# A decoder layer on one core: FFN tile 0 as plain products, partial sums of the other tiles in PSUM, and a final norm without GpSimd

## The chip, the core and the metric

The kernel runs on one core of a Trainium2 chip. The core's engines, as the profile names them, are TensorE (PE for matmuls and transposes, PEld for its weight loads), VectorE (DVE), ScalarE (ACT), GpSimd (POOL) and SyncE (SP, which here issues the DMAs). PE writes into PSUM banks; DVE and ACT read them. Each engine works through its own queue in order and waits on the others by semaphores. The metric is the device time of one execution, in microseconds (us).

## What is computed

One layer of a hybrid decoder on 512 tokens of width 1024, in float32. The part that the change touches is the last third:

```python
    x = x + jnp.concatenate([y_attn, y_ssd, y_pool], axis=-1) @ w_out
    h = rmsnorm(x, norm_ffn)
    gate, up = jnp.split(h @ w_gate_up, 2, axis=-1)
    return x + (jax.nn.silu(gate) * up) @ w_down
...
    return rmsnorm(x, norm_final)
```

`FFN_HIDDEN` is 2816, so the feed-forward part (FFN) has 22 tiles of 128 hidden units. What comes ahead (a norm, the input projection, block-sparse attention, a state-space scan and a pooling mixer) is the same in both kernels.

## The kernel before

**Precision.** Every float32 operand is split into a high part (a copy by ACT into the matmul type) and a low part (source minus high part, on DVE; `hi_lo`, lines 809 and 810). `mm3` issues three matmuls for one product of 128 rows: high x high (line 166), high x low (167) and low x high (168). So every product counts three times.

**The boundary.** The output projection writes `po0` and `po1` (512 columns each) for four token tiles t of 128 tokens. `add_x1` (766) adds them to x on DVE, `square` (774) gives the row sums on ACT, `row_rstd` (780 to 787) turns them into the norm's factor by a short chain of 128x1 instructions on DVE with a Sqrt on ACT in it. `h2_lane(t)` then makes `xh` (932, two halves on DVE), has PE transpose it into two banks `ps_h` (939, eight transposes), and splits the banks into `h2_hi` (950, ACT) and `h2_lo` (951, DVE). Token tiles 2 and 3 also make the sums `t1` to `t4` of four quadrants of the normalised rows (966 to 974, DVE), each split into a high and a low part (962, 963); three of them are the operands `T2`, `T3`, `T4`, the fourth goes in place of a quadrant of `h2_hi`.

**The tiles.** For each hidden tile, gate and up, for both halves of the tokens (256 each) and both halves of the inner dimension (512 each), are computed by a Strassen-Winograd scheme: seven products instead of eight, of four steps x three matmuls of 256 columns, so 12 matmuls each and 84 for a tile. They are numbered 1, 2, 6, 7, 5, 4, 3, in that order (`pair_order`). Their weights are a gate tile (products 1 and 2), a half of an up tile (4), and sums of those (`add_up`, 856 to 859, on DVE): `sa` for 5 and 6, `sb` for 7 and 3. `block` issues one product into its half of a bank (`psf1`, `psf2`, `psf7`, `psf5`, `psf4`; 2 and 6 share one, 4 and 3 another). `block_out` adds up: ACT copies product 1 out (1064), DVE does six adds in a buffer `E` (1059: one of 512 columns, five of 256), ACT does one Silu over 512 columns (1080), DVE the product (1081), and `hi_lo` makes `aTh` and `aTl`.

**Groups.** Tiles come in the groups of `GROUPS`: 0 to 3, 4 to 7, 8 to 11, 12 to 15, 16 and 17, 18 to 21. After each the down projection multiplies the group's tiles into `pd` (512 columns, four token tiles, two output halves h) and DVE adds that to x. In the first group, products 1 and 2 of tiles 0, 1 and 2 (`FIRST`, line 38) stand ahead of the rest, since they need only the first 256 tokens.

**The end.** The last half of the last group is `pdl`, token tile by token tile, the last one in two parts of 256 columns. Each is added to x on DVE (1169), squared on ACT (1172), multiplied by the final norm's weights `gf` on GpSimd (1151 for the left half, 1174 for the right), given its factor by `row_rstd`, scaled on ACT (left, 1180) and DVE (right, 1182), and written by two DMAs from SP (1181, 1183).

**What sets the order.** A scheduler places each instruction in its engine's queue by program order, with those under `high_priority` ahead. Weight loads (512 KB each, four raw buffers) and their splits are drawn from the list `plan` by `advance`, one or more after each product, when a slot is free and the load has landed by the planner's own clock. `issue_after` forces an instruction behind a given one. `H2_DELAY` (39) is how far each `h2_lane` waits on the planner's clock before its transposes.

## Time and profile before

| | |
|---|---|
| median of 3 runs (lowest to highest) | 577.88 us (576.05 to 577.88) |
| the profiled execution, device time | 577.72 us |
| its span in the profile | 576.0 us |
| PE busy | 557.9 us, 3492 matmuls and transposes |
| DVE busy | 463.0 us |
| ACT busy | 281.0 us |
| GpSimd busy | 60.1 us |
| data read from and written to memory | 58.93 MB, 2.11 MB |

The span is the time from the first to the last instruction that the profiler records. "Busy" counts the time in which an engine works, not the time in which it waits for a semaphore. Matmuls overlap in the pipeline: each shows its full duration (0.28 us for 256 columns), and the next one starts 0.12 us after it. So PE's pace is read from starts, not from durations.

### The profile page before, as it was taken

Reading aid. Unit: us, or ns where it says so; the run is one execution under the profiler, and the core shown is the slowest. Engines: PE = TensorE matmul, PEld = TensorE weight load, DVE = VectorE, ACT = ScalarE, POOL = GpSimd, SP = SyncE. Lnnn points to the kernel's source line nnn. Section 1 sums busy time; section 2 is a strip of 40 time slices with the busy share of each in tenths; the row PEclk is TensorE's granted clock in tenths of the full one; section 3 lists DMA queues with packets and bytes.
Section 4 is the critical chain, followed back from the end, with each engine's and each line's share of the span. In section 5 each row is a group of like instructions: output and inputs, shape, how many; then the busy total and the mean of one; then the engine's idle time right before and its main releaser. Section 6 shows DMA issues by size and latency. Waiting matters only on the chain.

```text
span 576.0 us, 9083 instructions
## 1 busy us (share of the span) xinstructions
PE 557.9 (97%) x3492; PEld 501.6 (87%) x3492; DVE 463.0 (80%) x838; ACT 281.0 (49%) x481; POOL 60.1 (10%) x75
## 2 busy tenths in 40 slices
PE   7999999999998997999999999999999999999994
PEld 4998998888776886998899989998899889899984
DVE  4387966899989768999899968897689877798445
ACT  5686554667646546464345522643155324325234
POOL 6011002006860000000000000000000000000033
PEclk8999999999999998999999999999999999999998
DMA  7862233422122701245324321443034233222003
GB/s 238 296 209 75 74 109 110 129 75 86 43 75 73 292 0 38 74 126 175 138 75 147 115 106 47 156 128 110 0 121 162 85 109 110 75 73 75 1 0 146
DMA packets 19519, 61.62 MB, mean 107 GB/s; under 512 B 2300, under 2 KB 3476, under 8 KB 19476
## 3 DMA queue, kind: packets, MB, share of 16 engines
q1 hardware_dynamic: 19476, 61.05, 31.6%
q8 instruction: 27, 0.44, 0.3%
q14 instruction: 16, 0.13, 0.1%
HBM read 58.93 MB, written 2.11 MB: 106 GB/s over the span
## 4 chain that ended last, share of the span: by engine, by line
PE 61%; DVE 7%; ACT 1%; issue 1%; DVEq 0%; ACTq 0%
PE psf L166 12%; PE psf L168 11%; PE psf L167 11%; PE pd L166 6%; PE pd L167 6%; PE pd L168 6%; PE po L166 2%; PE po L167 2%; PE po L168 2%; PE ps_h L939 1%; DVE sl L810 1%; DVE E L1059 1%; DVE x L1169 0%; DVE sz L528 0%; ACT sqf L1172 0%
## 5 line engine op out<-in xcount | busy, mean ns | idle before, releaser
L167 PE MATMUL pd<-dl,aTh 128*128 128x512 f32 x160 | 63.3, 395 | 0.0
L166 PE MATMUL pd<-dh,aTh 128*128 128x512 f32 x160 | 62.8, 396 | 0.0
L168 PE MATMUL pd<-dh,aTl 128*128 128x512 f32 x160 | 60.8, 395 | 0.0
L1059 DVE TENSOR_TENSOR E<-psf,E 128x256 f32<-128x256 f32 x110 | 42.4, 418 | 11.2 <-PE psf L168 10.3
L166 PE MATMUL psf<-h_hi,gh 128*128 128x256 f32 x176 | 49.9, 285 | 0.1
L167 PE MATMUL psf<-h_lo,sh 128*128 128x256 f32 x176 | 49.7, 282 | 0.0
L167 PE MATMUL psf<-h_lo,gh 128*128 128x256 f32 x176 | 49.7, 283 | 0.0
L168 PE MATMUL psf<-h_hi,gl 128*128 128x256 f32 x176 | 49.6, 282 | 0.0
L168 PE MATMUL psf<-h_hi,sl 128*128 128x256 f32 x176 | 49.5, 281 | 0.0
L166 PE MATMUL psf<-h_hi,sh 128*128 128x256 f32 x176 | 49.5, 281 | 0.0
L138 DVE TENSOR_TENSOR wlo<-raw,whi 128x1024 fp32r<-128x1024 f32 (+3 forms) x29 | 33.6, 1159 | 18.0 <-ACT whi L137 17.9
L1151 POOL TENSOR_TENSOR x<-x,gf 128x512 f32<-128x512 f32 x4 | 5.1, 1294 | 359.5 <-ACT sqf L774 359.5
L137 ACT ACTIVATE whi<-raw 128x1024 fp32r<-128x1024 f32 (+3 forms) x34 | 31.6, 931 | 22.0 <-PE pc L167 10.0
L166 PE MATMUL pc<-hT_hi,whi 128*128 128x512 f32 x104 | 41.3, 397 | 0.0
L809 ACT ACTIVATE sh<-sb 128x1024 fp32r<-128x1024 f32 x22 | 23.2, 1056 | 36.3 <-PE pd L167 29.8
L168 PE MATMUL pc<-hT_hi,wlo 128*128 128x512 f32 x104 | 40.9, 393 | 0.0
L167 PE MATMUL pc<-hT_lo,whi 128*128 128x512 f32 x104 | 40.8, 392 | 0.0
L766 DVE TENSOR_TENSOR x<-pd,x 128x512 f32<-128x512 f32 x44 | 28.4, 686 | 14.9 <-PE pd L168 14.8
L809 ACT ACTIVATE dh<-r_d 128x1024 fp32r<-128x1024 f32 x22 | 23.1, 1057 | 33.9 <-PE psf L167 22.6
L168 PEld LDWEIGHTS pd<-dh,aTl 128*128 128x128 f32 x160 | 30.1, 188 | 7.3
L166 PEld LDWEIGHTS pd<-dh,aTh 128*128 128x128 f32 x160 | 30.1, 188 | 7.0
L167 PEld LDWEIGHTS pd<-dl,aTh 128*128 128x128 f32 x160 | 30.1, 188 | 6.9
(291 smaller groups left out, 1714.3 us busy)
## 6 DMA issues: line engine op xcount, KB each, us to landing
r_g<-wgu SPq DMA_DIRECT2D x22, 512.0 KB, 3.7
r_u<-wgu SPq DMA_DIRECT2D x22, 512.0 KB, 3.9
r_d<-wd SPq DMA_DIRECT2D x22, 512.0 KB, 3.2
raw<-w SPq DMA_DIRECT2D x13, 512.0 KB, 3.5
raw<-wo SPq DMA_DIRECT2D x8, 512.0 KB, 3.2
rawx<-xT SPq DMA_DIRECT2D x8, 256.0 KB, 3.8
rawn<-xn SPq DMA_DIRECT2D x4, 512.0 KB, 5.1
x<-xn SPq DMA_DIRECT2D x4, 512.0 KB, 7.2
```

The source lines that it names most:

```text
L137: nc.scalar.activation(hi[:, sl], raw[:, sl], AF.Copy)
L138: eng.tensor_tensor(lo[:, sl], raw[:, sl], hi[:, sl].bitcast(F32), ALU.subtract)
L166: nc.tensor.matmul(ps, s_hi, m_hi, start=first, stop=False)
L167: nc.tensor.matmul(ps, s_hi, m_lo, start=False, stop=False)
L168: nc.tensor.matmul(ps, s_lo, m_hi, start=False, stop=last)
L766: nc.vector.tensor_tensor(x1[t][:, cs], ps, x1[t][:, cs], ALU.add)
L809: nc.scalar.activation(hi, src, AF.Copy)
L810: eng.tensor_tensor(lo, src, hi.bitcast(F32), ALU.subtract)
L939: nc.tensor.transpose(pst[:, j * P : (j + 1) * P], xh[:, kt * P : (kt + 1) * P], ident)
L1059: nc.vector.tensor_tensor(o_, a_, b_, ALU.add)
L1151: nc.gpsimd.tensor_tensor(x1[t][:, :512], x1[t][:, :512], gf[0][:, :512], ALU.mult)
```

## The change

**Tile 0 plain.** Tile 0 is computed as eight plain products: `g0`, `u0` (gate and up of the first 256 tokens) and `g1`, `u1` (the other half), each of 24 matmuls of 256 columns into banks `pspg` and `pspu`. The new order of the first group is g0, u0 of tile 0, then products 1 and 2 of tiles 1, 2 and 3, then g1, u1, then the rest. Their weights need only the split, no sums. The loads come in the same order.

**The boundary.** All four token tiles now split both halves into `h2_hi` and `h2_lo` and copy both out, `xh` has two buffers, the sums of quadrants are made in place and are no longer under `high_priority`, and the fourth sum has an operand `T1` of its own (product 5 reads it).

**Sums in PSUM.** In tiles 1 to 21 products 1, 6, 7 and 4 are accumulated in one bank `psB`, one after the other; products 5 and 3 likewise in `psC`; product 2 has `psA`. ACT copies the partial sum out of `psB` after product 1 (`u1`), 6 (`u2`) and 7 (`u3`); DVE adds each of them once to another bank. The Silu is done in two halves of 256 columns. `pair_order` puts products of the next tile between those of a tile, and products 4 and 3 of a group's last tile go into the down projection, ahead of its second tile.

**The end.** The products with `gf` move from GpSimd to DVE, on the right into the scaling itself. The factor's chain (`last_rstd`) lets the Sqrt read the sum of squares with scale and bias, so that one step ahead of it falls away. The Sqrt's table is loaded right behind the last Silu (`pre2`). The left half's DMA is issued from ACT's queue, the right half of the last token tile goes in two parts, and the last matmuls are held in program order.

The diff, cut to its core:

```diff
-FIRST = [(i, n) for i in range(3) for n in (1, 2)]
-H2_DELAY = (10.0, 5.0, 3.0, 3.0)
...
+PLAIN = (0,)
+EARLY = (1, 2, 3)
+FIRST = (
+    [(i, n) for i in PLAIN for n in ("g0", "u0")]
+    + [(i, n) for i in EARLY for n in (1, 2)]
+    + [(i, n) for i in PLAIN for n in ("g1", "u1")]
+)
+H2_DELAY = (7.0, 5.0, 5.0, 5.0)
...
+        def left_out(t, r):
+            nc.scalar.activation(x1[t][:, :512], x1[t][:, :512], AF.Copy, scale=r)
+            nc.scalar.dma_start(out[t * P : (t + 1) * P, :512], x1[t][:, :512])
+
+        def last_rstd(t):
+
+            y = tiny.tile([P, 1], F32, name=f"rsfy{t}", tag="rsy")
+            v = tiny.tile([P, 1], F32, name=f"rsfv{t}", tag="rsv")
+            a = tiny.tile([P, 1], F32, name=f"rsfa{t}", tag="rsa")
+            root[t] = nc.scalar.activation(y, ss[:, t, 1:2], AF.Sqrt, scale=1.0 / D, bias=ss[:, t, 0:1]).ins
+            nc.vector.scalar_tensor_tensor(v, ss[:, t, 1:2], -0.5 / D, sh[:, t : t + 1], ALU.mult, ALU.add)
+            nc.vector.reciprocal(y, y)
+            nc.vector.tensor_scalar(a, y, y, v, ALU.mult, ALU.mult)
+            nc.vector.tensor_scalar(y, a, 1.5, y, ALU.add, ALU.mult)
+            return y
...
-                if gi == 0 and i == 0:
-                    stages[3:3] = [("wx", 2, split_g, 1), ("wx", 2, split_g, 2)]
-                elif gi == 0 and i in (1, 2):
+                if i in PLAIN:
+                    stages = [("wx", 2, split_plain, i, "g"), ("wx", 2, split_plain, i, "u")]
+                    if i == PLAIN[-1]:
+                        stages += [("wx", 2, split_g, k) for k in EARLY]
+                elif i in EARLY:
                     stages = stages[1:]
...
+
+            f_ = {1: b11, 3: b12, 2: b22, 4: b21}
+
+            def out_(n):
+                d_hi, d_lo = T[n][0][:, :, cs], T[n][1][:, :, cs]
+                nc.scalar.activation(d_hi, f_[n], AF.Copy)
+                return nc.vector.tensor_tensor(d_lo, f_[n], d_hi.bitcast(F32), ALU.subtract)
+
+            nc.vector.tensor_tensor(b11, b11, b12, ALU.subtract)
+            nc.vector.tensor_tensor(b12, b22, b12, ALU.subtract)
+            nc.vector.scalar_tensor_tensor(b22, b11, -1.0, b22, ALU.mult, ALU.subtract)
+            out_(2)
+            nc.vector.scalar_tensor_tensor(b21, b22, -1.0, b21, ALU.mult, ALU.subtract)
+            out_(3)
+            last = out_(1)
+            out_(4)
             crit.append(last.ins)
...
-                        h2_split(t, 1, b22)
+                for b in range(2):
+                    p3 = h2_bank(t, b, xh)
+                    h2_split(t, b, p3)
+                    h2_copy(t, b, p3)
+            mark(f"h2_{t}", 0.5)
             if t >= 2:
                 yield when("T")
-                with tc.high_priority():
-                    if t == 2:
-                        h2_sums(t, h2f[2, 0], h2f[2, 1])
-                    else:
-                        h2_sums(t, b12, b22)
-                        h2_split(t, 1, b22)
-            mark(f"h2_{t}", 0.5)
+                h2_sums(t)
+                mark(f"T_{t}", 0.5)
...
-        def block_out(i, n, e, ps):
-            if n == 1:
-                e["p1"] = fw.tile([P, 256], F32, name=f"p1_{i}", tag="p1", bufs=3)
-                nc.scalar.copy(e["p1"], ps)
...
+            gl, gr, ur = slice(0, 256), slice(256, 512), slice(256, 512)
+            if n in (1, 6, 7):
+                u_ = e["u1" if n == 1 else "u2" if n == 6 else "u3"] = (fw if n == 1 else ap_).tile(
+                    [P, 256], F32, name=f"u{n}_{i}", tag=f"u{n}", bufs=len(EARLY) + 1 if n == 1 else 2
+                )
+                nc.scalar.copy(u_, e["B"])
+            elif n == 2:
+                e["g"] = fw.tile([P, S], F32, name=f"g{i}", tag="g", bufs=4)
+                add(e["g"][:, gl], e["A"], e["u1"])
+                nc.scalar.activation(e["g"][:, gl], e["g"][:, gl], AF.Silu)
+            elif n == 4:
+                e["a"] = e.get("a") or ap_.tile([P, S], F32, name=f"a{i}", tag="a")
+                nc.vector.scalar_tensor_tensor(e["a"][:, :256], e["B"], -1.0, e["g"][:, gl], ALU.mult, ALU.mult)
...
+                add(e["g"][:, gr], e["C"], e["u2"])
+                last = nc.scalar.activation(e["g"][:, gr], e["g"][:, gr], AF.Silu)
+                if i == FT - 1:
+
+                    with tc.issue_after(last.ins):
+                        nc.scalar.activation(tiny.tile([P, NT], F32, name="pre2", tag="pre"), rstd, AF.Sqrt)
+                nc.vector.scalar_tensor_tensor(e["a"][:, ur], e["ur"], -1.0, e["g"][:, gr], ALU.mult, ALU.mult)
+                out_aT(i, e["a"])
                 st.pop(i)
+            if n in (5, 7) and "u3" in e and "C" in e:
+                e["ur"] = ap_.tile([P, 256], F32, name=f"ur{i}", tag="ur")
+                add(e["ur"], e["C"], e["u3"])
...
+            which = {1: "B", 6: "B", 7: "B", 4: "B", 2: "A", 5: "C", 3: "C"}[n]
+            new = which not in e
+            if new:
+                e[which] = bank(f"ps{which}_{i}")[:, :256]
+            ps = e[which]
             for kt in range(4):
                 sl = slice(kt * P, (kt + 1) * P)
-                mm3(ps, w_hi[:, sl], w_lo[:, sl], *moving(n, kt), kt == 0, kt == 3)
+                mm3(ps, w_hi[:, sl], w_lo[:, sl], *moving(n, kt), new and kt == 0, kt == 3, chain=not new)
...
+        def block_plain(i, what):
+
+            which, half = what[0], int(what[1])
+            need((i, which))
+            w_hi, w_lo = ops[i, which]
+            if (i, which) not in plain:
+                plain[i, which] = bank(f"psp{which}_{i}")
+            ts_ = slice(half * 256, (half + 1) * 256)
+            for kt in range(KT):
+                sl = slice(kt * P, (kt + 1) * P)
+                mm3(plain[i, which][:, ts_], w_hi[:, sl], w_lo[:, sl], h2_hi[:, kt, ts_], h2_lo[:, kt, ts_], kt == 0, kt == KT - 1)
+            if half:
+                ops.pop((i, which))
+                done("wx", 2)
+
+        def plain_out(i):
+            g = fw.tile([P, S], F32, name=f"g{i}", tag="g", bufs=4)
+            a_ = ap_.tile([P, S], F32, name=f"a{i}", tag="a")
+            nc.scalar.activation(g, plain[i, "g"], AF.Silu)
+            nc.vector.tensor_tensor(a_, plain[i, "u"], g, ALU.mult)
+            out_aT(i, a_)
...
-            return [(i, n) for i in range(lo_, hi_) for n in (1, 2, 6, 7, 5, 4, 3)]
+
+            tiles = [i for i in range(lo_, hi_) if i not in PLAIN]
+            order = []
+            for i, nxt in zip(tiles, tiles[1:] + [None]):
+                if (i, 6) not in order:
+                    order += [(i, n) for n in (1, 2, 6, 5, 7) if (i, n) not in order and (i, n) not in FIRST]
+                if nxt is None:
+                    return order, [(i, 4), (i, 3)]
+                if nxt in EARLY:
+                    order += [(nxt, 6), (i, 4), (nxt, 5), (i, 3), (nxt, 7)]
+                else:
+                    order += [(nxt, 1), (i, 4), (nxt, 2), (i, 3)]
...
-                seq = FIRST + [q for q in seq if q not in FIRST]
+                seq = FIRST + seq
             for j, q in enumerate(seq):
-                if gi == 0 and j == 6:
+                if q == (PLAIN[0], "g1"):
                     ensure("h2_2", "h2_3")
+                if gi == 0 and j == len(FIRST):
+                    ensure("T_2", "T_3")
                     L.drain()
-                    tfctx.close()
                     bctx.close()
                     ap_ = fpool("aT", 2)
-                block(*q)
+                    for i in PLAIN:
+                        plain_out(i)
...
+                            if h == 0 and k == lo_ + 1:
+                                for q in tail:
+                                    block(*q)
...
-                            nc.gpsimd.tensor_tensor(x1[t][:, :512], x1[t][:, :512], gf[0][:, :512], ALU.mult)
+                            nc.vector.tensor_scalar_mul(sh[:, t : t + 1], ss[:, t, 0:1], -0.5)
+                            nc.vector.tensor_tensor(x1[t][:, :512], x1[t][:, :512], gf[0][:, :512], ALU.mult)
...
+                                with tc.issue_after(pd_end):
+                                    pd_end = mm3(ps[:, part], aT[k][0][:, ts_], aT[k][1][:, ts_], w_hi[:, js], w_lo[:, js], k == lo_, k == hi_ - 1)
...
-                            r = row_rstd(t, "rsf")
-                        nc.scalar.activation(x1[t][:, :512], x1[t][:, :512], AF.Copy, scale=r)
-                        nc.sync.dma_start(out[t * P : (t + 1) * P, :512], x1[t][:, :512])
-                        nc.vector.tensor_scalar_mul(x1[t][:, 512:], x1[t][:, 512:], r)
-                        nc.sync.dma_start(out[t * P : (t + 1) * P, 512:], x1[t][:, 512:])
+                            r = last_rstd(t)
+                            if t > 0:
+                                with tc.issue_after(root[t]):
+                                    left_out(t - 1, rs[t - 1])
+                            rs[t] = r
+                            for part in parts:
+                                os_ = slice(512 + part.start, 512 + part.stop)
+                                nc.vector.scalar_tensor_tensor(x1[t][:, os_], x1[t][:, os_], r, gf[0][:, os_], ALU.mult, ALU.mult)
+                                nc.sync.dma_start(out[t * P : (t + 1) * P, os_], x1[t][:, os_])
+                            if t == NT - 1:
+                                left_out(t, r)
```

Three places of the order of instructions, first the kernel before, then the changed one; in the names, the digits right behind the letters are the token tile or the hidden tile, and the last number is a buffer's.

DVE at the boundary, between the transposes of token tile 2 and the second half of `xh` of tile 3 (`tf`, `T2l` to `T4l` are the sums and their low parts of tile 2). Before:

```order
L963 TENSOR_TENSOR h2_lo_2096<-tf12_2377,h2_hi_2095 128x4x128
L963 TENSOR_TENSOR T3l_2367<-tf32_2379,T3h_2366 128x4x128
L963 TENSOR_TENSOR T2l_2365<-tf22_2378,T2h_2364 128x4x128
L787 TENSOR_SCALAR rsay3_2395<-rsaa3_2396,rsay3_2395 128x1
L963 TENSOR_TENSOR T4l_2369<-tf42_2380,T4h_2368 128x4x128
L932 SCALAR_TENSOR_TENSOR xh3_2402<-x1_3_2074,rsay3_2395,gn_2075 128x512 x2
```

The changed kernel:

```order
L796 TENSOR_SCALAR rsay3_2358<-rsaa3_2359,rsay3_2358 128x1
L991 TENSOR_TENSOR h2_lo_2097<-ps_h20_2371,h2_hi_2096 128x4x128
L972 SCALAR_TENSOR_TENSOR xh3_2365<-x1_3_2074,rsay3_2358,gn_2075 128x512 x2
L991 TENSOR_TENSOR h2_lo_2097<-ps_h21_2380,h2_hi_2096 128x4x128
L1004 TENSOR_TENSOR h2f00_2252<-h2f00_2252,h2f20_2378 128x512
L1005 TENSOR_TENSOR h2f20_2378<-h2f21_2387,h2f20_2378 128x512
L1002 TENSOR_TENSOR T1l_2345<-h2f00_2252,T1h_2344 128x4x128
```

`xh3` moved ahead of the sums of token tile 2; the sums stand behind it.

ACT in the third group of tiles, between products of tiles 8 and 9 (`p1` and `u1`, `u6`, `u7` are copies out of a bank; `gh`, `vh`, `sh` are high parts of weights of tiles 10 and 11). Before:

```order
L1064 COPY p1_8_3774<-psf1_8_3761 128x256
L809 ACTIVATE gh10_3789<-r_g_10_3637 128x1024
L809 ACTIVATE vh10_3844<-r_u_10_3642 128x512
L809 ACTIVATE sh010_3862<-sa10_3807 128x1024
L1080 ACTIVATE E8_3805<-E8_3805 128x512
L1064 COPY p1_9_3903<-psf1_9_3890 128x256
```

The changed kernel:

```order
L1085 COPY u1_8_3781<-psB_8_3768 128x256
L836 ACTIVATE gh10_3799<-r_g_10_3644 128x1024
L1089 ACTIVATE g8_3796<-g8_3796 128x256
L836 ACTIVATE vh10_3838<-r_u_10_3661 128x512
L1085 COPY u6_8_3815<-psB_8_3768 128x256
L836 ACTIVATE sh010_3888<-sa10_3817 128x1024
L1085 COPY u1_9_3872<-psB_9_3859 128x256
L836 ACTIVATE gh11_3931<-r_g_11_3695 128x1024
L1089 ACTIVATE g9_3905<-g9_3905 128x256
L1085 COPY u7_8_3855<-psB_8_3768 128x256
```

Between two splits of weights there is now a copy or half a Silu, where there were several splits in a row.

PE at the end of the group of tiles 16 and 17, the last matmuls of one product of tile 17 and those that follow. Before:

```order
L166 MATMUL psf5_17_5274<-h2_hi_2095,sh017_5000 128x256
L167 MATMUL psf5_17_5274<-h2_lo_2096,sh017_5000 128x256
L168 MATMUL psf5_17_5274<-h2_hi_2095,sl017_5001 128x256
L166 MATMUL psf4_17_5294<-T4h_2368,vh17_4994 128x256
L167 MATMUL psf4_17_5294<-T4l_2369,vh17_4994 128x256
L168 MATMUL psf4_17_5294<-T4h_2368,vh17_4994 128x256
```

The changed kernel:

```order
L173 MATMUL psB_17_5199<-T3h_2348,sh117_5052 128x256
L174 MATMUL psB_17_5199<-T3l_2349,sh117_5052 128x256
L175 MATMUL psB_17_5199<-T3h_2348,sl117_5053 128x256
L173 MATMUL psB_17_5199<-T4h_2350,vh17_5026 128x256
L174 MATMUL psB_17_5199<-T4l_2351,vh17_5026 128x256
L175 MATMUL psB_17_5199<-T4h_2350,vh17_5026 128x256
```

Product 4 was in another bank than the product ahead of it; now it follows product 7 in the same bank, with no matmul between.

## Rows read from the trace of the kernel before

**Rows 1.** The page: the span, and each engine's busy time.

```profile
span 576.0 us, 9083 instructions
PE 557.9 (97%) x3492; PEld 501.6 (87%) x3492; DVE 463.0 (80%) x838; ACT 281.0 (49%) x481; POOL 60.1 (10%) x75
```

**Rows 2.** Windows of 16 us in the tiles: columns as the first line names them.

```profile
core 0: us, PE busy (x) PEld busy (x) DVE busy (x) ACT busy (x) POOL busy (x), PEclk, DMA share, GB/s
368.00:384.00 16.00, 16.00 (x137) 16.00 (x136) 14.79 (x25) 8.68 (x12) 0.00 (x0) 1.00 0.53 178
528.00:544.00 16.00, 16.00 (x137) 16.00 (x137) 9.31 (x16) 3.76 (x6) 0.00 (x0) 1.00 0.01 2
```

**Rows 3.** Windows of 4 us at the boundary, same columns.

```profile
224.00:228.00 4.00, 1.36 (x7) 1.35 (x8) 3.46 (x7) 0.23 (x1) 0.00 (x0) 0.83 0.00 0
228.00:232.00 4.00, 4.00 (x28) 4.00 (x27) 3.52 (x6) 3.35 (x6) 0.00 (x0) 0.74 0.40 133
```

**Rows 4.** Timeline of PE, boundary to the first group's end: start, duration, instruction, [wait].

```profile
209.96 0.39 PE L166 MATMUL po<-whi,mixT_hi 128*128 128x512 f32 x1
...
210.64 1.03 PE L939 MATMUL ps_h<-ident,xh 128*128 128x128 f32 x8
211.43 0.48 PE L166 MATMUL po<-whi,mixT_hi 128*128 128x512 f32 x1
...
216.33 1.03 PE L939 MATMUL ps_h<-ident,xh 128*128 128x128 f32 x8
...
218.21 1.32 PE L939 MATMUL ps_h<-ident,xh 128*128 128x128 f32 x8 [0.85 <-DVE xh L932]
...
219.72 0.28 PE L167 MATMUL psf<-h_lo,gh 128*128 128x256 f32 x1
...
223.51 0.28 PE L168 MATMUL psf<-h_hi,gl 128*128 128x256 f32 x1
...
226.64 1.97 PE L939 MATMUL ps_h<-ident,xh 128*128 128x128 f32 x8 [2.85 <-DVE xh L932]
...
287.62 0.28 PE L166 MATMUL psf<-h_hi,gh 128*128 128x256 f32 x1
```

**Rows 5.** Timeline of DVE at the boundary.

```profile
205.73 0.68 DVE L766 TENSOR_TENSOR x<-po,x 128x512 f32<-128x512 f32 x1
...
206.57 1.42 DVE L932 SCALAR_TENSOR_TENSOR xh<-x,rsay,gn 128x512 f32<-128x512 f32 x2
...
208.89 0.21 DVE L787 TENSOR_SCALAR rsay<-rsaa,rsay 128x1 f32<-128x1 f32 x1
...
232.50 0.68 DVE L856 TENSOR_TENSOR sa<-r_u 128x512 f32<-128x512 f32 x1
...
233.10 0.69 DVE L810 TENSOR_TENSOR vh<-r_u,vh 128x512 fp32r<-128x512 f32 x1
```

**Rows 6.** Instructions grouped by line, with busy total and mean ns: sums, copies of the tiles.

```profile
L1059 DVE TENSOR_TENSOR E<-psf,E 128x256 f32<-128x256 f32 x110 | 42.4, 418 | 11.2 <-PE psf L168 10.3
...
L1064 ACT COPY p<-psf 128x256 f32<-128x256 f32 x22 | 8.2, 374 | 28.4 <-PE psf L168 28.4
```

**Rows 7.** Timeline of the end, all engines.

```profile
561.48 1.28 ACT L783 ACT_TABLE_LOAD   x1
...
562.78 0.20 ACT L783 ACTIVATE rsfy<-rsfv 128x1 f32<-128x1 f32 x1
...
567.79 1.23 DVE L780 SCALAR_TENSOR_TENSOR rsfv<-ss 128x1 f32<-128x1 f32 x1
...
568.07 0.27 PE L168 MATMUL pdl<-dh,aTl 128*128 128x256 f32 x1
...
568.93 0.41 DVE L1169 TENSOR_TENSOR x<-pdl,x 128x256 f32<-128x256 f32 x1
...
571.10 0.33 SPq L1183 DMA_DIRECT2D out<-x  x1
```

**Rows 8.** DMA of the end: GB/s in 40 slices of 556 to 576 us.

```profile
GB/s 0 0 0 0 0 0 0 0 0 0 0 0 0 0 0 0 0 0 25 373 369 283 0 0 74 369 361 246 0 0 0 41 381 385 385 381 373 152 0 0
```

131 lines of the change are left out of this document (47 added, 84 removed).

## The prediction

> **What bounds the kernel now.** I began with the span line and the busy shares [rows 1]: TensorE (PE) is at work for 557.9 of 576.0 us, so an edit is worth only what it takes out of PE's queue, out of PE's few stops, or out of the two ends. Then the windows of the steady part: 368 to 384 and 528 to 544 us are 16.00 busy of 16.00 on PE, while VectorE (DVE) is at 14.79 and 9.31 and ScalarE (ACT) at 8.68 and 3.76 [rows 2]. In the FFN tiles DVE and ACT have time to spare, and relieving them there buys nothing by itself.
>
> Where does PE stop? Before the FFN's first group it does, twice, both times for `xh`, the normalised rows that it transposes: 0.85 us ahead of token tile 2, 2.85 us ahead of tile 3 [rows 4]. After the long stop the granted clock is down: a mean of 0.83 in 224 to 228 us and of 0.74 in the next 4 us, against 1.00 elsewhere [rows 2, 3]. The third place is the end: PE's last matmul ends at 568.07 + 0.27 = 568.34, the span at 576.0.
>
> My sum is made against this profiled execution: span 576.0, device time 577.72, so 1.72 us lie around the span. The median of the runs shown, 577.88, is 0.16 above it.
>
> **The boundary and the first group, before.** From 209.96 to 287.62 are 77.66 us [rows 4]. The work in it by its own pace: 120 matmuls of 512 columns at 0.233 (21 of them from 211.43 to 216.33) are 28.0; 336 of 256 columns (4 tiles of 84) at 0.1184 (32 from 219.72 to 223.51) are 39.8; four sets of eight transposes at 0.79 (210.64 to 211.43) are 3.2. Together 71.0, so 6.7 are lost. I can place 0.85 + 2.85 as waits for `xh`, and about 1.9 at the low clock: the eight transposes after the stop take 1.97 instead of 0.79 [rows 4], and 228 to 232 holds 28 matmuls [rows 3] where 4.00 / 0.1184 = 34 fit (6 x 0.12 = 0.7). Some 1.1 I cannot place, and I leave it in.
>
> **The same place, after.** Tile 0 is now eight plain products of 24 matmuls, half their weights ready early. The new order puts 16 transposes, 24 matmuls of `po1`, then 14 + 34 plain ones ahead of the transposes of token tile 3, and on DVE it puts the sums `T` behind `xh3`, not ahead of it. Does `xh3` come in time? The chain is the one that token tile 1 ran undisturbed: add at 205.73, root done at 208.89 + 0.21 = 209.10, two halves of `xh` in 1.42 [rows 5], 4.8 us in all. In the new order the last `po1` matmul ends at 209.96 + 16 transposes (1.58) + 24 x 0.233 = 217.1. So `xh3` is due near 222.0, some 0.4 later if the `h2_lo` that the order puts between slips in first. PE comes to its transposes at 217.1 + 48 x 0.1184 + 0.79 = 223.6. That leaves 1.2 to 1.6 us to spare; both waits should go, and with the long stop the low clock behind it. Gain 0.85 + 2.85 + 1.9 = 5.6.
>
> The cost in matmuls: 96 instead of 84 for tile 0, 12 x 0.1184 = +1.4. The cost in queues: DVE gets two more `h2_lo` halves, and all sums, of 512 columns, behind one another, with weight splits of 1024 columns among them. From 222 I count in the order 28 instructions of 512 columns at a pace of 0.60 (232.50 to 233.10 [rows 5]), three of 256 taken for half and two of 1024 for two each: 16.8 + 0.9 + 2.4 = 20.1, 21 with waits. The weight sum of tile 2 then ends near 243 and ACT's split of it near 244. PE is through the transposes of token tile 3 at 224.4 and has 156 matmuls before the product that takes this split, so it wants it at 242.9: a new wait of 1.1, with small ones 1.4 (bounds 0, if DVE waits less than I allow, and 3.5, below). Net for the boundary: 5.6 - 1.4 - 1.4 = 2.8. I take 3.0, since one wait that is off by a few tenths is as likely to shrink as to grow and part of the 1.1 should go with the stop.
>
> **The chains in PSUM.** Products 1, 6, 7, 4 of a tile now add up in one bank, and ACT copies the partial sum out between them. That trades DVE's adds (110 at 418 ns) for ACT's copies: 22 before at 374 ns [rows 6], three for each of 21 tiles after, so +41 x 0.374 = 15.3 us on ACT. By the windows ACT has that room. What counts is the order: the next product on the bank must wait until the copy is out. In steady groups the new order puts at least 24 matmuls, 2.8 us, between a product and its successor on the bank. Copy and its lags want about 0.6, so 2.2 us are left for what stands ahead of it in ACT's queue: a split of 1024 columns or a shorter one. I cost the steady groups at 0. If a copy had no cover, it would cost the drain of the last matmul (0.28 - 0.12 = 0.16), 0.374 and some 0.1 of hand-over, 0.63 each. Exactly one place has no cover: at the end of the group of tiles 16 and 17, where product 4 follows product 7 of tile 17 at once. That is +0.5 to +0.6 (0, if the copy's place in the trace hides in a neighbour; 1.0, if ACT is at a split): +0.5.
>
> In the last group the Sqrt table is now loaded right after the last Silu, ahead of the split that makes `aTh` of tile 21. A load takes 1.28 us and the instruction behind it starts at once: 561.48 + 1.28 = 562.76, next at 562.78 [rows 7]. Fifteen matmuls of the down projection, 3.5 us, cover it; I get readiness 3.55 after product 3: +0.1. The Trainium skill ("ScalarE: Activation LUTs", What ACT_TABLE_LOAD costs) adds a drain of some 1.4 us to the load; by it the term would be +1.5, but the row shows none behind the load.
>
> **The end.** Before, DVE's add of the last quarter starts at 568.93, 0.59 after PE is through, because a 128x1 instruction on DVE sits there for 1.23 us from 567.79 while GpSimd multiplies; elsewhere the like takes about 0.2 (208.89) [rows 5, 7]. With GpSimd's products gone, so is that. The norm's chain is shorter by one DVE step, the table is there, and the output's right half of token tile 2 should be issued 1.55 after PE's end (before: 571.10 - 568.34 = 2.76 [rows 7]). From there 576.0 - 571.10 = 4.9 us remained, most of it transfer: the last 1 MB at 373 to 385 GB/s [rows 8] is 2.75 us. I keep the 4.9: 1.55 + 4.9 = 6.45 in place of 7.66, -1.2. Bounds -0.6 (the left half, now issued from ACT's queue, goes late behind a square) and -1.8 (transfers start with gaps closed).
>
> **Sum.** -3.0 + 0.5 + 0.1 - 1.2 = -3.6: span 572.4, profiled time 574.1; the median of such runs likewise near 574.1 to 574.3. I say **574.1**.
>
> **Rivals.** *The chains hold PE (slower).* ACT stands in a split of 1024 columns, or waits in one for a buffer, and one copy in each of the 21 tiles is late with its full 0.63: 13.2 us, so 574.1 + 13.2 = 587. It decides from 5.5 us over the whole, that is 0.26 in each tile. Against it: ACT is at 8.68 of 16 in the busiest window [rows 2], and the cover is 2.8 us. For it: a single queue in order, and 41 more instructions in it, each with a wait. *The stop comes back inside the first group (same).* DVE is full from 222 to 243 in my own count, and a delay of 2 us more in front of the weight sum makes PE stand for over 2.85 us, with the low clock behind it as before (1.9 [rows 3, 4]): +3.5 on my 1.4, 577.6. For it: DVE's extra sums, that the order of weight splits in the first group has no slack. Against it: my count has PE waiting for 1.1 only. *No wait at all (on my side):* the 1.4 of waits and the 1.1 unplaced are gone too, 574.1 - 2.5 = 571.6.
>
> **How the numbers follow.** About 0.3%, 1.7 us, is what a measurement of this kernel can tell from none: faster is under 576.15, slower over 579.6. My forecast with its spread (0 to 3.5 at the boundary, 0 to 1.0 at tile 17, 0.6 to 1.8 at the end) has 0.57, no wait at all 0.20: both faster, 0.77. The stop inside the first group has 0.15: same. The chains hold PE: 0.08, slower. The range reaches from just below the case without waits to just above the stop's, 571.2 to 577.8; it leaves out the 0.08 and a few hundredths at either end.
>
> **What would show it.** Right: no wait for `xh` at the transposes of token tile 3 and a granted clock of 1.00 in 224 to 232 us; PE at 16.00 of 16.00 in the steady windows with three copies in each tile; one idle place of about 0.6 at product 4 of tile 17; the last DMA issue 3 us after PE's last matmul, no GpSimd there. Wrong: waits of `psB` for the copy in tile after tile; a stop over 2 us between 230 and 250 with a low clock after it; a wait for `aTh` of tile 21; an end over 7 us after PE's last matmul.

## The result, and the profile after

The changed kernel takes 572.30 us (median of 4 runs, 572.24 to 573.43) against 577.88 us before: a ratio of 0.9914, 95% interval 0.9893 to 0.9936. The prediction was 574.1 in a range of 571.2 to 577.8. The profiled execution took 572.36 us with a span of 570.6, 5.4 less than the 576.0 of before.

The page after, span and busy shares (compare [rows 1]):

```profile
span 570.6 us, 9068 instructions
PE 557.1 (98%) x3504; PEld 502.7 (88%) x3504; DVE 434.9 (76%) x792; ACT 299.0 (52%) x545; POOL 49.8 (9%) x66
```

PE does 12 matmuls more and is busy 0.8 us less; its share goes from 97% to 98%. DVE has 28 us less to do, ACT 18 us more, GpSimd 10 less.

Windows of 4 us at the boundary (columns as in [rows 2]), to be held against [rows 3]:

```profile
224.00:228.00 4.00, 4.00 (x36) 4.00 (x35) 4.00 (x8) 3.69 (x9) 0.00 (x0) 1.00 0.02 8
228.00:232.00 4.00, 4.00 (x35) 4.00 (x35) 3.77 (x9) 3.97 (x8) 0.00 (x0) 1.00 0.02 4
...
240.00:244.00 4.00, 3.17 (x25) 2.92 (x25) 4.00 (x7) 2.52 (x5) 0.00 (x0) 1.00 0.00 0
```

PE is full from 224 to 232 us at a granted clock of 1.00, where it stood for most of 4 us before and then ran at 0.74. The only window with a gap is 240 to 244. PE's timeline shows why, and the other places where it waits in the FFN (start, duration, instruction, [wait]):

```profile
217.94 1.03 PE L979 MATMUL ps_h<-ident,xh 128*128 128x128 f32 x8
...
222.89 1.03 PE L979 MATMUL ps_h<-ident,xh 128*128 128x128 f32 x8
...
243.56 0.39 PE L173 MATMUL psB<-T2h,sh 128*128 128x256 f32 x1 [0.83 <-ACT sh L836]
...
486.50 0.28 PE L175 MATMUL psB<-T3h,sl 128*128 128x256 f32 x1
487.24 0.39 PE L173 MATMUL psB<-T4h,vh 128*128 128x256 f32 x1 [0.46 <-ACT u L1085]
487.46 0.28 PE L174 MATMUL psB<-T4l,vh 128*128 128x256 f32 x1
...
501.46 0.39 PE L173 MATMUL psB<-h_hi,gh 128*128 128x256 f32 x1 [0.18 <-DVE x L775]
```

Both transposes of `xh` start without a wait ([rows 4] had 0.85 and 2.85). There is 0.83 for the high part of tile 2's weight sum, 0.46 for the copy `u7` of tile 17, 0.18 at the start of the last group. In the steady groups the timeline marks no wait at all. (At the start of the last group PE stood for 0.12 before, so that one is hardly new.)

The last rows say how to price a wait. Before the wait at 487.24 the matmul at 486.50 would have been followed after 0.12; it was followed after 0.74, and the next came 0.22 later, not 0.12. So a wait that the trace shows as 0.46 costs 0.62 + 0.10 = 0.72: a wait's idle time is counted from the end of the matmul ahead (0.28 after its start), and PE starts slower behind it. Some 0.26 come on top of each wait shown.

The end, all engines, against [rows 7]:

```profile
563.97 0.28 PE L175 MATMUL pdl<-dh,aTl 128*128 128x256 f32 x1
...
564.28 0.42 DVE L1241 TENSOR_TENSOR x<-pdl,x 128x256 f32<-128x256 f32 x1 [0.49 <-PE pdl L175]
...
565.66 2.05 SPq L1258 DMA_DIRECT2D out<-x  x3
...
567.36 0.35 ACTq L803 DMA_DIRECT2D out<-x  x1
```

PE is through at 563.97 + 0.28 = 564.25. The add of the last quarter starts 0.03 later (0.59 before), the right half of token tile 2 is issued after 1.41 (2.76 before), the last DMA after 3.11, and the end comes 6.35 us after PE's (7.66 before).

Stage by stage, from the starts of the first matmuls of each stage on PE:

| stage | before | after | difference | forecast |
|---|---|---|---|---|
| start to the last `po1` | 209.96 | 209.06 | -0.90 | 0 |
| boundary and first group | 77.66 | 73.92 | -3.74 | -3.0 |
| groups 2 to 4, each | 62.25 | 62.12 | -0.40 in all | 0 |
| group of tiles 16 and 17 | 31.41 | 32.12 | +0.71 | +0.5 |
| last group, to PE's end | 62.55 | 62.79 | +0.24 | +0.1 |
| end | 7.66 | 6.35 | -1.31 | -1.2 |
| sum | 576.0 | 570.6 | -5.4 | -3.6 |

In the changed kernel the first stretch ends at the 16 transposes that now stand ahead of `po1`, so the second holds the same work as before but for tile 0's 12 matmuls. Every term that was not forecast at 0 has the sign that was forecast. What was not forecast are 0.90 ahead of the change, 0.40 in groups whose matmuls are of the same number and size, and 0.7 more at the boundary. The experiments went for these.

### The profile page after: what moved, and what is told of

The parts are those of the page before. It is cut to its first block, busy times and chain, and to the rows that moved or that the text cites. A ratio compares the mean times of both kernels' runs of the same rounds, so it can differ in the third digit from the quotient of the medians.

```text
span 570.6 us, 9068 instructions
## 1 busy us (share of the span) xinstructions
PE 557.1 (98%) x3504; PEld 502.7 (88%) x3504; DVE 434.9 (76%) x792; ACT 299.0 (52%) x545; POOL 49.8 (9%) x66
## 4 chain that ended last, share of the span: by engine, by line
PE 65%; DVE 2%; ACT 1%; issue 0%; ACTq 0%; DVEq 0%
PE psB L173 7%; PE psB L175 7%; PE psB L174 7%; PE pd L173 6%; PE pd L174 6%; PE pd L175 6%; PE psC L175 3%; PE psC L174 3%; PE psC L173 3%; PE po L173 2%; PE po L174 2%; PE po L175 2%; PE psA L175 2%; PE psA L174 2%; PE psA L173 2%; PE pdl L175 1%
## 5 line engine op out<-in xcount | busy, mean ns | idle before, releaser
L173 PE MATMUL pd<-dh,aTh 128*128 128x512 f32 x160 | 61.5, 391 | 0.0
L175 PE MATMUL pd<-dh,aTl 128*128 128x512 f32 x160 | 58.6, 389 | 0.0
L837 DVE TENSOR_TENSOR gl<-r_g,gh 128x1024 fp32r<-128x1024 f32 x22 | 27.0, 1226 | 15.7 <-ACT gh L836 9.9
L1085 ACT COPY u<-psB 128x256 f32<-128x256 f32 x63 | 23.0, 365 | 29.0 <-PE psB L175 28.3
L836 ACT ACTIVATE gh<-r_g 128x1024 fp32r<-128x1024 f32 x22 | 23.3, 1058 | 22.3 <-DMA r_g<-wgu 10.5
L837 DVE TENSOR_TENSOR sl<-sa,sh 128x1024 fp32r<-128x1024 f32 x21 | 25.6, 1221 | 11.1 <-PE psA L174 10.4
L837 DVE TENSOR_TENSOR sl<-sb,sh 128x1024 fp32r<-128x1024 f32 x21 | 25.6, 1218 | 10.5 <-ACT sh L836 7.3
L836 ACT ACTIVATE sh<-sa 128x1024 fp32r<-128x1024 f32 x21 | 22.3, 1060 | 15.9 <-DVE sa L887 9.5
L837 DVE TENSOR_TENSOR dl<-r_d,dh 128x1024 fp32r<-128x1024 f32 x22 | 26.8, 1219 | 4.7 <-ACT dh L836 4.7
L173 PE MATMUL po<-whi,mixT_hi 128*128 128x512 f32 x64 | 25.4, 399 | 1.9 <-ACT mixT_hi L309 1.5
```

The lines of the kernel that those rows point to most:

```text
L173: nc.tensor.matmul(ps, s_hi, m_hi, start=first, stop=False, skip_group_check=chain)
L175: last_mm = nc.tensor.matmul(ps, s_lo, m_hi, start=False, stop=last, skip_group_check=chain)
L836: nc.scalar.activation(hi, src, AF.Copy)
L837: eng.tensor_tensor(lo, src, hi.bitcast(F32), ALU.subtract)
L1085: nc.scalar.copy(u_, e["B"])
```

## Experiments

**Start addresses.** The groups' 0.40 is the sum of two larger things. Before, 256-column matmuls follow one another after 0.1186 us and `pd`'s of 512 columns after 0.2333 (means over some 1,780 and 450 starts); after, 0.1199 and 0.2275. The change puts one more small tile (`sh`) into the pool ahead of the weights, and all pools behind it move by 32 bytes. So I moved them in both kernels, with tiles that hold nothing.

```diff
+        pad = x1p.tile([P, 1], F32, name="pad")
+        nc.vector.memset(pad, 0.0)
         wxp = fpool("wx", 10)
```

> The kernel before with one unused 128x1 tile more ahead of the weight pool, so that the weights' tiles and aT start at a multiple of 64 bytes, as in the changed kernel (before: 32 past one). Theory A, the start addresses set the pace of the matmuls: 256-column matmuls go from a pitch of 0.1186 to 0.1200 us (some 1,320 of them, +2.2 us), the 480 of pd from 0.2333 to 0.2269 (-3.1), together -0.9 us against before. Rival B, the pace follows what the other engines do (DVE is busy for 80% before, 76% after): both pitches stay, 0 us. In both, the first stretch up to the output projection tells whether its 0.9 us differ between executions of the same instructions.

576.13 us, ratio to before 0.9977 (0.9964 to 0.9989). Starts on PE: the second group, its `pd`, the third group, in the kernel before and then in this one:

```profile
327.48 0.40 PE L166 MATMUL pd<-dh,aTh 128*128 128x512 f32 x1
...
349.87 0.28 PE L166 MATMUL psf<-h_hi,gh 128*128 128x256 f32 x1
```

```profile
287.03 0.28 PE L166 MATMUL psf<-h_hi,gh 128*128 128x256 f32 x1
...
327.35 0.40 PE L166 MATMUL pd<-dh,aTh 128*128 128x512 f32 x1
...
349.13 0.28 PE L166 MATMUL psf<-h_hi,gh 128*128 128x256 f32 x1
```

From 287.62 [rows 4] to 327.48 are 336 matmuls, 39.86 / 336 = 0.1186, and 96 of `pd` in 22.39, 0.2332 each. With the unused tile it is 40.32 / 336 = 0.1200 and 21.78 / 96 = 0.2269: the changed kernel's paces, in the kernel before, with the same instructions in the same order. So theory A held and B fell. By these paces the FFN gains only 0.6 of the 1.7 us. Some 0.4 more go with the granted clock (see the end): of the 49 executions of the kernel before whose mean granted clock is on record beside these runs, the 20 at 0.993 or more took 577.0 us in the mean and the other 29 took 578.0; of this kernel's ten, eight were at 0.993 or more. The rest is not settled.

The same tile in the changed kernel:

```diff
+        pad = x1p.tile([P, 1], F32, name="pad")
+        nc.vector.memset(pad, 0.0)
         wxp = fpool("wx", 10)
```

> The changed kernel with the same unused tile, so that weights and aT start 32 bytes past a multiple of 64, as before the change. A: 256-column pitch 0.1200 to 0.1185 (some 1,350, -2.0 us), pd 0.2269 to 0.2333 (+3.1), so +1.1 us against the changed kernel's 572.3. B: no change, 572.3.

571.44 us (ratio 0.9898, 0.9876 to 0.9920), 0.9 less than the changed kernel, where I had expected 1.1 more. `pd` went back to 0.2334 as expected, but the 256-column matmuls went to 0.1175 on average and to 0.1167 where the weights are in the moved pool, beyond the 0.1185 that I had taken from before.

One more in the pool behind the weights, so that aT moves by 64 bytes and the weights by 32:

```diff
+        pad = x1p.tile([P, 1], F32, name="pad")
+        nc.vector.memset(pad, 0.0)
...
         fw = fpool("fwork", 2)
+        pad2 = fw.tile([P, 1], F32, name="pad2", tag="pad2", bufs=1)
+        nc.vector.memset(pad2, 0.0)
```

> The changed kernel with two such tiles: the weights start 32 past a multiple of 64, aT on a multiple. A: 256-column pitch 0.1185 and pd 0.2269, the better of both: -2.0 us, 570.3. B: 572.3.

569.78 us (0.9883, 0.9851 to 0.9914): as A said. 256 columns at 0.1176, `pd` at 0.2288.

Then the kernel before with two such tiles ahead of the weights and seven more ahead of aT, the first of each shown:

```diff
+        pad0 = x1p.tile([P, 1], F32, name="pad0")
...
+        qad0 = fw.tile([P, 1], F32, name="qad0", tag="qad0", bufs=1)
...
```

> The kernel before, with nothing changed but the start addresses: the weights at 96 past a multiple of 256 bytes, aT at 128 past one, the offsets that had the best pace for each so far (0.1167 for 256 columns, 0.227 for pd). If the offset sets the pace: some 1,320 matmuls by -0.0016 and 480 by -0.006, -5.0 us, 572.8, the changed kernel's time. If it is not the offset but something else of the layout: within 575 to 578.

573.00 us, ratio 0.9914 (0.9892 to 0.9936). Starts on PE at the same three places:

```profile
286.88 0.28 PE L166 MATMUL psf<-h_hi,gh 128*128 128x256 f32 x1
...
326.39 0.40 PE L166 MATMUL pd<-dh,aTh 128*128 128x512 f32 x1
...
348.19 0.28 PE L166 MATMUL psf<-h_hi,gh 128*128 128x256 f32 x1
```

39.51 / 336 = 0.1176 and 21.80 / 96 = 0.2271. The kernel before, moved by 64 and 288 bytes and not otherwise changed, comes within 0.7 us of the changed kernel.

**Order alone.** Is it enough to let `xh3` go ahead of the sums?

```diff
...
+                if t == 2:
+                    yield 3.0
                 with tc.high_priority():
                     if t == 2:
-                        h2_sums(t, h2f[2, 0], h2f[2, 1])
+                        with tc.issue_after(xh_end[3]):
+                            h2_sums(t, h2f[2, 0], h2f[2, 1])
```

> The kernel before with one thing changed: the sums of token tile 2 are held behind xh of tile 3 on DVE. PE's order stays. My account: xh3 is ready near 222.3 us, PE reaches its transposes at 223.7, so the stop of 2.85 us and the low clock behind it (1.9) go; the sums are late in return, and PE waits some 2 us at the first product that takes T2, near 229 us: -2.5 to -3 us in the boundary. Rival: without the plain tile's 48 matmuls the stop only moves to the T2 product at full length (over 2.85 us) with a low clock behind it: 0 us, within 0.5.

577.90 us, ratio 1.0000 (0.9987 to 1.0013): the rival's time. PE's waits behind the transposes of token tile 3, which themselves start without one, and two windows:

```profile
229.83 0.38 PE L166 MATMUL psf<-T2h,sh 128*128 128x256 f32 x1 [1.22 <-ACT T2h L963]
...
230.43 0.39 PE L166 MATMUL psf<-T3h,sh 128*128 128x256 f32 x1 [0.22 <-ACT T3h L963]
...
233.91 0.39 PE L167 MATMUL psf<-T2l,sh 128*128 128x256 f32 x1 [1.68 <-DVE T2l L964]
...
248.13 0.39 PE L168 MATMUL psf<-T2h,sl 128*128 128x256 f32 x1 [0.89 <-DVE sl L810]
```

```profile
228.00:232.00 4.00, 2.56 (x20) 2.15 (x18) 4.00 (x7) 2.33 (x5) 0.00 (x0) 1.00 0.00 0
232.00:236.00 4.00, 2.32 (x19) 2.12 (x19) 4.00 (x8) 0.63 (x1) 0.00 (x0) 1.00 0.00 0
```

The stop is gone, and 1.22 + 0.22 + 1.68 + 0.89 have come in its place, each with its 0.26. The granted clock stays at 1.00, so the rival's mechanism (one stop at full length, with a low clock) did not come; its time did. DVE is busy for 4.00 of 4.00 in both windows: whatever PE does not wait for at the transposes, it waits for at the products that take the sums.

**Less cover.** In the changed kernel, products 1 and 2 of tile 3 no longer go early.

```diff
-EARLY = (1, 2, 3)
+EARLY = (1, 2)
```

> The changed kernel with products 1 and 2 of tiles 1 and 2 only, not of tile 3, ahead of the second half of tile 0: 24 matmuls (2.9 us) less cover while DVE makes the sums. My account: DVE is the limit there, so the wait for the high part of the weight sum of tile 2 grows from 0.83 to about 3.3 us, +2.5: 574.8; if so long a stop brings the low clock back, +1.9 more, 576.7. Rival: DVE is not the limit in that stretch and the wait stays under 1: 572.3.

573.91 us (0.9945, 0.9927 to 0.9963), 1.6 more than with three early tiles. The waits in that stretch:

```profile
238.21 0.39 PE L175 MATMUL psB<-T2h,sl 128*128 128x256 f32 x1 [1.11 <-DVE sl L837]
...
243.44 0.38 PE L173 MATMUL psB<-T2h,sh 128*128 128x256 f32 x1 [0.84 <-ACT sh L836]
```

A second wait of 1.11 (1.4 with its 0.26) has come ahead of the 0.84, which has not grown. DVE ends that wait, so it is the limit there, but the price was 1.6 where I had expected 2.5: not all of the 2.9 us of missing cover arrives as waits. The clock stayed up.

**Bare copies.** The first attempt put products 1, 6 and 7 one after the other in `pair_order`.

```diff
-                    order += [(nxt, 1), (i, 4), (nxt, 2), (i, 3)]
+                    order += [(i, 4), (i, 3)]
...
-                    order += [(i, n) for n in (1, 2, 6, 5, 7) if (i, n) not in order and (i, n) not in FIRST]
+                    order += [(i, n) for n in ((1, 6, 7, 2, 5) if i not in EARLY else (1, 2, 6, 5, 7)) if (i, n) not in order and (i, n) not in FIRST]
```

> The changed kernel with products 1, 6 and 7 of each tile from 4 to 21 directly one after the other, so that two copies out of the bank in each tile, 36 in all, have no matmul to hide behind. By the one such place in the changed kernel (tile 17, 0.46 us of wait, 0.7 longer in all): +25 us, 597. By the price in my prediction, 0.63 each: +23. Rival: ACT stands in a split when the copy is due, which makes each dearer by half a split: over 1.2 each, +43 or more. If copies cost nothing even bare: 572.3.

573.18 us (0.9933, 0.9912 to 0.9953), and inconclusive: the scheduler had put the products between again, and PE's waits were the changed kernel's three (0.83, 0.46, 0.18). The 0.9 us more lie ahead of the change: `po` starts 1.1 later. The second attempt keeps that order and holds each product behind the one ahead:

```diff
+                with tc.issue_after(mm_end[0]) if i >= 4 and mm_end[0] is not None else ExitStack():
-                mm3(ps, w_hi[:, sl], w_lo[:, sl], *moving(n, kt), new and kt == 0, kt == 3, chain=not new)
+                    mm_end[0] = mm3(ps, w_hi[:, sl], w_lo[:, sl], *moving(n, kt), new and kt == 0, kt == 3, chain=not new)
...
```

> As the run with bare copies, but now each product from tile 4 on is held behind the one ahead of it in PE's queue, since the scheduler had put the others between again. 36 copies then have no matmul to hide behind. By the one such place in the changed kernel (0.46 us of wait, 0.7 longer): +25 us, 597. By my prediction's price, 0.63: +23. Rival: ACT stands in a split when the copy is due: over 1.2 each, +43 or more. If copies cost nothing even bare: 572.3.

604.71 us, ratio 1.0468 (1.0446 to 1.0489), 32.4 more than the changed kernel. PE's waits (engine, line, waited for: us in total, times, longest):

```profile
PE psB L173 <- ACT u L1085: 19.9, 36, 1.1
PE psC L173 <- DVE ur L1077: 1.6, 1, 1.6
...
PE pd L173 <- ACT aTh L836: 1.4, 1, 1.4
```

36 waits of 0.55 on average, 0.81 with the 0.26: 29.3 of the 32.4, and the two other rows are about the rest. So my price of 0.63 lacked the restart, and ACT does stand in something else at times (the longest is 1.1). The rival that put 13 us on the change (21 copies at 0.63) was, if anything, low in its price per copy; the interleaved order is what kept it away.

**GpSimd alone.** The products with `gf` moved to DVE in the kernel before, nothing else:

```diff
-                            nc.gpsimd.tensor_tensor(x1[t][:, :512], x1[t][:, :512], gf[0][:, :512], ALU.mult)
+                            nc.vector.tensor_tensor(x1[t][:, :512], x1[t][:, :512], gf[0][:, :512], ALU.mult)
...
-                            nc.gpsimd.tensor_tensor(xs_, xs_, gf[0][:, gs], ALU.mult)
...
-                        nc.vector.tensor_scalar_mul(x1[t][:, 512:], x1[t][:, 512:], r)
+                        nc.vector.scalar_tensor_tensor(x1[t][:, 512:], x1[t][:, 512:], r, gf[0][:, 512:], ALU.mult, ALU.mult)
```

> The kernel before with one part of the new end alone: the products with the final norm's weights go from GpSimd to DVE, the right half's into its scaling. My account: the 128x1 instruction that stood on DVE for 1.23 us while GpSimd multiplied takes about 0.2, the add of the last quarter starts at once, and the end behind PE's last matmul goes from 7.66 to about 6.9 us, some 0.7 less; the other 0.6 of the changed kernel's gain belong to the shorter chain of the norm and its second queue. Rival: the 1.23 us has nothing to do with GpSimd; it stays, and the end stays at 7.66 or grows by DVE's products.

576.85 us, ratio 0.9992 (0.9976 to 1.0007): too small for the clock on the wall, but plain in the trace:

```profile
567.38 0.15 DVE L780 SCALAR_TENSOR_TENSOR rsfv<-ss 128x1 f32<-128x1 f32 x1
...
568.05 0.42 DVE L1169 TENSOR_TENSOR x<-pdl,x 128x256 f32<-128x256 f32 x1 [0.52 <-PE pdl L168]
```

The 128x1 instruction that took 1.23 us in [rows 7] takes 0.15, and the last quarter's add starts 0.04 after PE's end at 568.01. The span is 575.2, so the end takes 7.19 in place of 7.66: 0.47 of the 1.31 belong to GpSimd, 0.84 to the rest of the new end (the shorter chain, the second queue, the right half in two parts), which was not tried apart. In the two runs of the kernel before with unused tiles the unchanged end took 7.77, so 0.1 either way is noise.

**The three waits taken away.** `plain_out(0)` is held on DVE behind the low part of tile 2's weight sum; product 5 of tile 17 is held between its products 7 and 4; the Sqrt's table is loaded behind `aTh` of tile 21. And three unused tiles stand ahead of the weights, one more ahead of aT, where they were expected to give the good paces.

```diff
-                    for i in PLAIN:
-                        plain_out(i)
...
+                if q == (2, 6):
+                    with tc.issue_after(lo_ins[2, 0]):
+                        plain_out(0)
...
+                order += [(b, 1), (a, 4), (b, 2), (b, 6), (a, 3), (b, 7), (b, 5)]
+                return order, [(b, 4), (b, 3)]
...
-                out_aT(i, e["a"])
+                last = out_aT(i, e["a"])
+                if i == FT - 1:
+                    with tc.issue_after(last.ins):
+                        nc.scalar.activation(tiny.tile([P, NT], F32, name="pre2", tag="pre"), rstd, AF.Sqrt)
```

> The changed kernel with unused tiles that put the weights 32 past a multiple of 128 bytes and aT on one, and with its three remaining waits of the FFN taken away: DVE finishes tile 0 only after the weight sum of tile 2 (the wait of 0.83), a product of another bank stands between 7 and 4 of tile 17 (0.46), and the Sqrt table is loaded behind aTh of tile 21 (0.4). If an offset of 32 works like one of 96 (256-column pitch 0.1167): the run with padded weights' 569.8 less 1.8 to 2.2, about 567.8. If the kernel before's 0.1183 belongs to an offset of 32: 2.2 more, about 570.

574.06 us (0.9948, 0.9932 to 0.9964). The waits went (0.23 is left of the 0.83), and the paces were bad: 0.1198 and 0.2325, `pd` although aT starts on a multiple of 128 bytes. So neither a multiple of 64 nor one of 128 is the rule. In a table of all runs, with the offsets from a multiple of 256 bytes, only 128 for aT had given `pd` its 0.227, and 128 is where `pd`'s other operand, in the ring of weights, starts. The next run took 128 for aT and 96 for the weights.

It has the three edits above, with one unused tile ahead of the weights and seven ahead of aT in place of three and one:

```diff
-        pad1 = x1p.tile([P, 1], F32, name="pad1")
...
-        pad2 = x1p.tile([P, 1], F32, name="pad2")
...
+        qad1 = fw.tile([P, 1], F32, name="qad1", tag="qad1", bufs=1)
...
+        qad6 = fw.tile([P, 1], F32, name="qad6", tag="qad6", bufs=1)
```

> The changed kernel with its three waits of the FFN taken away, as in the mended run, and with the offsets 96 for the weights and 128 for aT. If the offset sets the pace: 569.8 of the run with padded weights, less 0.6 for pd, less 1.5 for the waits, 567.7. If not: about 571 to 574.

567.65 us, ratio 0.9826 (0.9812 to 0.9841): the fastest of all, 4.65 under the changed kernel and 10 under the kernel before. Starts of the third group, its `pd`, and the fourth group:

```profile
343.75 0.28 PE L173 MATMUL psB<-h_hi,gh 128*128 128x256 f32 x1
...
380.41 0.40 PE L173 MATMUL pd<-dh,aTh 128*128 128x512 f32 x1
...
405.08 0.28 PE L173 MATMUL psB<-h_hi,gh 128*128 128x256 f32 x1
```

312 matmuls in 36.66 are 0.1175 each. The last run moves the ring too.

```diff
+        wpad = wrp.tile([P, 56], F32, name="wpad", tag="wpad", bufs=1)
+        nc.vector.memset(wpad, 0.0)
+        hpad = hp.tile([P, 8], F32, name="hpad", tag="hpad", bufs=1)
+        nc.vector.memset(hpad, 0.0)
```

> The mended and shifted run with one thing more: the ring of tiles that holds the weights of products 7 and 3, the down projection's weights and the projections' weights starts at 96 past a multiple of 256 bytes, not 128. If a matmul's pace goes by the offset of its own stationary operand (the 128x128 that PE loads): products 7 and 3, some 500 matmuls, go from 0.1196 to 0.1167 (-1.5 us), the 300 of the projections ahead from 0.230 to 0.233 (+1.0), pd stays at 0.2275, since its stationary operand is aT: 567.2. If it goes by the distance between the stationary and the moving operand: pd, whose moving operand moves, changes too, to 0.233 as in other mismatches (+2.8): about 570.

570.67 us (0.9882, 0.9850 to 0.9914). The same three places:

```profile
345.99 0.28 PE L177 MATMUL psB<-h_hi,gh 128*128 128x256 f32 x1
...
382.39 0.40 PE L177 MATMUL pd<-dh,aTh 128*128 128x512 f32 x1
...
407.59 0.28 PE L177 MATMUL psB<-h_hi,gh 128*128 128x256 f32 x1
```

The 312 take 36.40, 0.1167, since products 7 and 3 now have it too. But from `pd`'s start to the next group it is 25.20 us, where it was 24.67 in the run before: `pd` is at 0.2335, with aT where it was. So the pace goes by both operands, not by the stationary one alone. The projections ahead went from 0.230 and 0.228 to 0.234.

## Why the prediction held, step by step

**The boundary: right in its mechanism, with three terms mis-sized.** The waits for `xh` and the low clock went, as said; 48 matmuls of the plain tile were cover enough, and the run with the order alone shows that without the plain tile the order gains nothing. (The plain tile without the new order was not run.) The new wait was forecast at 1.1, at 242.9 us, for the high part of tile 2's weight sum; it came at 243.56, for that, with 0.83 (1.1 with the restart). The small waits that I had added (0.3) did not come. I had the restarts at nothing: three waits before (0.85, 2.85, 0.22) at 0.26 each are 0.8, and the third wait itself was not in my sum either.

The low clock, at 1.9, was too dear. I had held the duration of the eight transposes behind the stop (1.97) against their time from start to start elsewhere (0.79), two different measures. The same 44 matmuls, from these transposes to the first with `T2h`, ended like this in the kernel before, and ran like this in the run with `gf` on DVE, where the same stop brought no low clock:

```profile
233.42 0.28 PE L166 MATMUL psf<-T2h,sh 128*128 128x256 f32 x1
```

```profile
226.78 1.38 PE L939 MATMUL ps_h<-ident,xh 128*128 128x128 f32 x8 [2.85 <-DVE xh L932]
...
232.26 0.28 PE L166 MATMUL psf<-T2h,sh 128*128 128x256 f32 x1
```

From 226.64 [rows 4] that is 6.78 against 5.48: the low clock cost 1.3. So what went is 0.85 + 2.85 + 0.22 + 0.8 + 1.3 = 6.0, not 5.6; less the 1.4 of matmuls and the 1.1 of the new wait it makes 3.5 of the 3.74. Of the 77.66 before, 0.6 stay open.

**The chains: right.** At like offsets the steady groups take 61.31 us with DVE's adds (348.19 - 286.88) and 61.33 with ACT's copies (405.08 - 343.75): the added copies cost nothing there, and DVE's relief brings nothing. The one bare place cost 0.71 for a forecast of 0.5; the term lacked the restart. In the first group one copy of the changed kernel, behind product 7 of tile 2 (251.05 to 251.42 on ACT), has only four matmuls for cover, about 0.48 us:

```profile
251.21 0.28 PE L174 MATMUL psC<-T1l,sh 128*128 128x256 f32 x1
251.47 0.38 PE L173 MATMUL psB<-T4h,vh 128*128 128x256 f32 x1
251.70 0.28 PE L174 MATMUL psB<-T4l,vh 128*128 128x256 f32 x1
```

The next product starts 0.14 late and 0.11 slower, though the timeline marks no wait: 0.25, about the bare price of 0.72 less the cover.

**The table: right in kind.** ACT and PE after:

```profile
548.11 1.28 ACT L1099 ACT_TABLE_LOAD   x1
549.40 0.21 ACT L1099 ACTIVATE pre<-rstd 128x4 f32<-128x4 f32 x1
...
549.84 0.39 PE L175 MATMUL pd<-dh,aTl 128*128 128x512 f32 x1
550.18 0.50 PE L173 MATMUL pd<-dh,aTh 128*128 128x512 f32 x1
550.51 0.40 PE L174 MATMUL pd<-dl,aTh 128*128 128x512 f32 x1
```

The load takes 1.28 us again and the instruction behind it starts at 549.40; `aTh` of tile 21 comes 0.11 late and PE restarts 0.10 slower, so 0.2 of the last group's 0.24 are this; I had 0.1, again without the restart. The Trainium skill ("ScalarE: Activation LUTs", What ACT_TABLE_LOAD costs) has a drain of some 1.4 us behind it, by which the term was +1.5: no run here shows one.

**The end: right.** 1.41 for a forecast of 1.55, 3.11 for 3.0, 6.35 for 6.45. The Trainium skill ("SBUF — State Buffer", Who interferes with whom) says that a DVE instruction with two inputs in SBUF contends with a GpSimd instruction that reads there; the 1.23 that became 0.15 agrees. One row does not fit so simply: in the kernel before, the same instruction took 0.15 at 570.05, beside a GpSimd product whose row begins at 570.02.

**What was missing.** The medians moved by 5.6 us where I forecast 3.8, and the part that I did not foresee could as well have gone the other way. First, 0.90 us ahead of the change are no gain that it made: in the thirteen executions profiled with the same instructions ahead of it, `po` starts anywhere from 157.96 (after) to 159.60 us (the first run with an unused tile). Second, the change carried something that its diff does not tell: 32 bytes, worth 0.6 by the paces. That both fell on the side of the gain is luck.

What is left of the 5.4 in the two profiled executions is 3.9, close to my 3.6. At like offsets it is less certain. Against the kernel before with the same offsets the medians give 3.8 (576.13 to 572.30), but of the 4.4 between the two traces 1.6 lie ahead of the change, and from the last `po1` on it is worth 2.7; neither trace has the low clock there. At the best offsets found, and with the low clock in the kernel before, the same stretch gives 3.2 (medians 3.2 too: 569.78 against 573.00), where `pd` had 0.0018 x 480 = 0.9 against it. So the change is worth some 4 us where the stop brings the low clock and some 2.7 where it does not; I had taken the low clock for granted.

## What to carry to other kernels

Where PE is full, a change moves time only through its stops and its ends; price a stop as the trace's idle time plus the restart, and ask which engine is the limit behind it, since a stop taken away at one place comes back at the next while that engine is full. A copy between two accumulations in one bank is free here with two products (2.8 us) of other banks between, and costs 0.7 to 0.8 us bare. Before two versions are compared, look whether their matmuls have the same pace from start to start: here, with the same matmuls in the same order, the pace changed with nothing but where the tiles start.
